# A 16 KB store of zeros, with two waits for it, at the start of a streaming subtract-the-mean kernel

## The chip, the cores and the metric

One core of one Trainium2 chip. The metric is the device time of one execution in microseconds (us); medians of several executions are given. Most executions of this kernel agree within some 0.3 us. The span of a profile is about 2 us shorter than the time of the same execution; times are compared with times and spans with spans.

## The reference

```python
B, S, D = 8, 4096, 2112          # x: float32
x_r = x.reshape(B, S // 4, 4, D)
pooled = x_r.mean(axis=2)
return x - np.repeat(pooled, 4, axis=1)
```

Four consecutive rows form a group; the mean of the group is taken from each of its rows. There are 8192 groups of 4 x 2112 = 8448 numbers. The kernel reads 276.8 MB and writes 276.8 MB.

## The kernel before

A tile is 128 groups, one per partition: 128 rows of 33,792 bytes. There are 64 tiles and six tile buffers ("slots"). SP (the sync engine) issues all loads, DVE (the vector engine) makes three adds and one fused subtract per tile, ACT (the scalar engine) issues all stores; SBUF and PSUM are the two on-chip memories. A load waits until the store that last used its slot has landed; the first six loads wait for nothing.

```python
for k in range(n):                                   # n = 64
    b, lap = k % SLOTS, k // SLOTS                   # SLOTS = 6
    load = nc.sync.dma_start(out=slots[b][:], in_=xg[k * P:(k + 1) * P])
    if lap:
        load._wait_ge(store_sems[b], 16 * lap)
    load.then_inc(load_sems[b], 16)
# ... DVE: for each tile three adds into s (s_sb in SBUF for even slots, s_ps in PSUM
#     for odd ones); the first add waits for load_sems[b]; then
#     slot = slot - s / 4, which raises done_sem ...
for k in range(n):
    b = k % SLOTS
    store = nc.scalar.dma_start(out=og[k * P:(k + 1) * P], in_=slots[b][:])
    store._wait_ge(done_sem, k + 1)
    store.then_inc(store_sems[b], 16)
```

## Time and profile before

| | before |
|---|---|
| time | 1284.66 us (6 runs beside the changed kernel, 1284.61 to 1284.79) |
| profiled span | 1283.3 us |
| DMA engines | full in all 40 slices |
| DVE | busy 80%, first add at 13.32 us |
| first store issued | 29.50 us |

The lines behind the table are in the prediction. One more view: what SP's loads wait for. Columns: who waited, for what, microseconds in total, how often, the longest.

```profile
SPq L85 <- DMA out_dram<-slot: 1169.0, 58, 50.7
```

Of the 64 loads 58 wait for a store to land, which makes the six slots a closed ring: load, compute, store, load again. While any load or store is queued, the 16 DMA engines have work.

The trace also holds the start, duration and size of every DMA packet. I sort the data packets by start and average each successive 16 of them, since 16 engines work side by side. In the kernel before, the median step from one such average to the next is 1.247 us: the time of one 33,792-byte row on one engine. 1024 rows per engine at 1.247 us are 1276.9 us of the 1283.3 us span, so the engines set the time.

### The profile page before, as it was taken

Reading aid. Unit: us, or ns where it says so; the run is one execution under the profiler, and the core shown is the slowest. Engines: PE = TensorE matmul, PEld = TensorE weight load, DVE = VectorE, ACT = ScalarE, POOL = GpSimd, SP = SyncE. Lnnn points to the kernel's source line nnn. Section 1 sums busy time; section 2 is a strip of 40 time slices with the busy share of each in tenths; the row PEclk is TensorE's granted clock in tenths of the full one; section 3 lists DMA queues with packets and bytes.
Section 4 is the critical chain, followed back from the end, with each engine's and each line's share of the span. In section 5 each row is a group of like instructions: output and inputs, shape, how many; then the busy total and the mean of one; then the engine's idle time right before and its main releaser. Section 6 shows DMA issues by size and latency. Waiting matters only on the chain.

```text
span 1283.3 us, 483 instructions
## 1 busy us (share of the span) xinstructions
DVE 1026.5 (80%) x256; POOL 0.2 (0%) x4
## 2 busy tenths in 40 slices
DVE  5998788787887877878778787787877878878785
POOL 0000000000000000000000000000000000000000
DMA  9999999999999999999999999999999999999999
GB/s 404 420 436 429 434 437 434 427 437 436 427 436 437 434 427 437 436 427 436 437 433 428 437 436 426 437 437 433 428 437 434 428 437 437 432 429 437 434 427 404
DMA packets 18432, 553.66 MB, mean 431 GB/s; under 512 B 2048, under 2 KB 2048, under 8 KB 2048
## 3 DMA queue, kind: packets, MB, share of 16 engines
q1 hardware_dynamic: 9216, 276.83, 50.1%
q10 hardware_dynamic: 9216, 276.83, 50.0%
HBM read 276.82 MB, written 276.82 MB: 431 GB/s over the span
## 4 chain that ended last, share of the span: by engine, by line
DVE 73%; another core or an unknown queue 24%; DMA 1%; issue 1%; DVEq 0%; SPq 0%
DVE slot L69 38%; DVE s_ps L63 18%; DVE s_sb L63 18%; DMA slot<-in_x_dram 1%; DVEq L90 0%; SPq L133 0%; SPq L82 0%
## 5 line engine op out<-in xcount | busy, mean ns | idle before, releaser
L69 DVE SCALAR_TENSOR_TENSOR slot<-s_sb,slot 128x8448 f32<-128x8448 f32 x32 | 286.7, 8958 | 1.1
L69 DVE SCALAR_TENSOR_TENSOR slot<-s_ps,slot 128x8448 f32<-128x8448 f32 x32 | 286.6, 8957 | 1.1
L63 DVE TENSOR_TENSOR s_sb<-slot 128x2112 f32<-128x2112 f32 x32 | 75.5, 2358 | 123.7 <-DMA slot<-in_x_dram 123.7
L63 DVE TENSOR_TENSOR s_ps<-slot 128x2112 f32<-128x2112 f32 x32 | 75.7, 2367 | 112.1 <-DMA slot<-in_x_dram 112.1
L63 DVE TENSOR_TENSOR s_ps<-s_ps,slot 128x2112 f32<-128x2112 f32 x64 | 151.4, 2366 | 2.2
L63 DVE TENSOR_TENSOR s_sb<-s_sb,slot 128x2112 f32<-128x2112 f32 x64 | 150.9, 2358 | 2.2
L122 POOL MEMSET const-bfloat16-1.0<- 128x1 bf16 x1 | 0.1, 102 | 0.0
L122 POOL MEMSET const-uint8-127<- 128x1 uint8 x1 | 0.1, 102 | 0.0
L122 POOL MEMSET const-float32-0.0<- 128x1 f32 x1 | 0.1, 99 | 0.2 <-issue 0.2
L122 POOL MEMSET const-float32-1.0<- 128x1 f32 x1 | 0.1, 99 | 0.0
## 6 DMA issues: line engine op xcount, KB each, us to landing
slot<-in_x_dram SPq DMA_DIRECT2D x64, 4224.0 KB, 60.1
out_dram<-slot ACTq DMA_DIRECT2D x64, 4224.0 KB, 43.5
```

The lines of the kernel that those rows point to most:

```text
L63: add = nc.vector.tensor_add(out=s[:], in0=first, in1=rows[:, f, :])
L69: sub = nc.vector.scalar_tensor_tensor(out=rows, in0=s[:, None, :].to_broadcast([P, STRIDE, D]), scalar=-1.0 / STRIDE, in1=rows, op0=mybir ...
L122: nc = _bacc.Bacc("TRN2", target_bir_lowering=False, num_devices=1)
```

## The change

A store of 32 rows of 512 bytes of zeros goes out first, into rows that the first tile's store overwrites. ACT waits for it to land before its first tile store (two writes to the same rows must not race), and DVE waits for it before its loop (it is going to overwrite the zeros in `s_sb`). The result is the same. Presumably the intent is to have the store queue used once before it matters; the code doesn't say.

```diff
+OPEN_ROWS, OPEN_COLS = 32, 128
 ...
+    open_sem = tc.alloc_semaphore("open")
+    opened = tc.alloc_semaphore("opened")
     with tc.tile_critical():
+        zeros = s_sb[:OPEN_ROWS, :OPEN_COLS]
+        nc.vector.memset(zeros, 0.0).then_inc(open_sem)
+        small = nc.scalar.dma_start(out=og[:OPEN_ROWS, :OPEN_COLS], in_=zeros)
+        small._wait_ge(open_sem, 1)
+        small.then_inc(opened, 16)
+        nc.scalar.wait_ge(opened, 16)
+        nc.vector.wait_ge(opened, 16)
         for k in range(n):
```

## The prediction

> **What bounds the kernel now.** I read the page first, then the waits, then the timeline of the first 70 us and a table of busy time by stretch. On the page the digits over 40 slices, the queues and the first DVE groups carry the reading:
>
> ```profile
> span 1283.3 us, 483 instructions
> DVE 1026.5 (80%) x256; POOL 0.2 (0%) x4
> DMA  9999999999999999999999999999999999999999
> GB/s 404 420 436 429 434 437 434 427 437 436 427 436 437 434 427 437 436 427 436 437 433 428 437 436 426 437 437 433 428 437 434 428 437 437 432 429 437 434 427 404
> DMA packets 18432, 553.66 MB, mean 431 GB/s; under 512 B 2048, under 2 KB 2048, under 8 KB 2048
> q1 hardware_dynamic: 9216, 276.83, 50.1%
> q10 hardware_dynamic: 9216, 276.83, 50.0%
> L69 DVE SCALAR_TENSOR_TENSOR slot<-s_sb,slot 128x8448 f32<-128x8448 f32 x32 | 286.7, 8958 | 1.1
> L63 DVE TENSOR_TENSOR s_sb<-slot 128x2112 f32<-128x2112 f32 x32 | 75.5, 2358 | 123.7 <-DMA slot<-in_x_dram 123.7
> ```
>
> The 16 DMA engines are full from the first slice to the last: the two queues' shares add up to 100.1% of 16 engines' span. Of the 18432 packets 2048 are tiny (the completion writes: 128 transfers by 16), so 16384 carry data, 1024 on each engine, and 1.001 x 1283.3 us / 1024 = 1.254 us is the mean time of one packet of 33,792 bytes (one row of a tile). DVE is busy 80% and waits for loads in between, so it isn't the bound. The chain of waits gives 73% to DVE; that is only the last link of each wait, and I overrule it with the DMA row, because the gaps on that chain are waits for transfers.
>
> The opening decides whether the change can touch anything. The timeline from 0 to 70 us:
>
> ```profile
> 0.95 53.96 SPq L85 DMA_DIRECT2D slot<-in_x_dram  x7
> 13.32 2.36 DVE L63 TENSOR_TENSOR s_sb<-slot 128x2112 f32<-128x2112 f32 x1 [13.32 <-DMA slot<-in_x_dram]
> ...
> 20.50 8.96 DVE L69 SCALAR_TENSOR_TENSOR slot<-s_sb,slot 128x8448 f32<-128x8448 f32 x1
> ...
> 29.50 32.45 ACTq L100 DMA_DIRECT2D out_dram<-slot  x3
> ```
>
> Loads start at 0.95 us, DVE is idle until 13.32 us, and ACT has no store to issue before 29.50 us. Everything that the change adds for DVE and ACT falls into these two idle stretches. The seventh load, the first that needs a store to have landed, is the last of the seven in the first line and goes out at about 0.95 + 53.96 = 54.9 us. The table by stretch shows that the engines don't run dry meanwhile:
>
> ```profile
> 0.00:10.00 10.00, 0.00 (x0) 0.20 (x4) 1.00 0.82 328
> 10.00:20.00 10.00, 6.61 (x3) 0.00 (x0) 1.00 1.00 433
> 30.00:40.00 10.00, 9.90 (x4) 0.00 (x0) 1.00 1.05 412
> 40.00:50.00 10.00, 9.97 (x3) 0.00 (x0) 1.00 1.00 433
> 50.00:60.00 10.00, 9.93 (x3) 0.00 (x0) 1.00 1.02 439
> ```
>
> The last two columns are DMA share and GB/s. Share 1.00 at 433 GB/s is the steady rate; the only dip inside is 412 GB/s in 30 to 40 us, when the first store joins the loads.
>
> **What the Trainium skill says.** (1) "DMA: Bandwidth & Descriptors", section "Where 436 GB/s comes from", puts the ceiling of a core's 16 ports at 435 GB/s. The trace agrees: 433 GB/s in full stretches. So there is no room for a faster kernel with the same bytes. (2) The same page, "Queues, rings and completion order": each engine alternates between queues with work, packet by packet. The trace agrees in its totals, 50.1% and 50.0% for the two queues, and the first store, issued at 29.50 us while loads were queued, had landed by 54.9 us, 25.4 us later. A store of 4224 KB (4.325 MB) at half of 433 GB/s takes 20.0 us; behind the queued loads it would have landed far later. (3) The same page, "Why a DMA increments its semaphore by 16 and not by 1": 32 rows are dealt to 16 engines, so two rows of 512 bytes and one completion write on each. (4) The same page, "Anatomy of one DMA", gives a fixed cost of about 2.0 us, mostly the receipt of the last write, for another path of issue than this one; the trace's nearest thing is the first load, issued at 0.95 us and seen at 13.32 us, 12.4 us where 4.325 MB at 433 GB/s take 10.0 us, so 2.4 us over the bytes. I use 2.4.
>
> **The change, part by part.** Nothing is removed and nothing is reordered: the comparison of the instruction streams shows one memset ahead of DVE's loop and one small store ahead of ACT's 64; the order on SP is the same.
> - Memset of 32x128 on DVE: four memsets of 128x1 on POOL take 0.1 us each; I take 0.1 to 0.2 us. It lies in the idle 13.32 us. Cost on the path: 0.
> - Small store: issued by ACT at some 1 to 2.5 us, after the memset. Each engine must pass two data packets and a completion write, with a load's packet of 1.254 us ahead of each: 3 x 1.254 = 3.8 us, plus 2.4 us fixed, plus up to one more packet already begun: 6 to 8 us. Landing at 8 to 10 us after the start. Estimate.
> - ACT's wait for it: over at 8 to 10 us, needed at 29.50 us: at least 19 us spare. Cost 0.
> - DVE's wait for it: over at 8 to 10 us, first load there at 13.32 us: 3 to 5 us spare. Cost 0. Should it miss by a few us, DVE and the first store start that much later, but two or more loads are still queued when the first store lands (54.9 - 2 us at 433 GB/s moved 22.9 MB, 5.3 tiles, of which at least one was a store and so at most 4.3 loads of 6). The engines have some 15 us or more of loads left, so a miss of a few us costs 0 too.
> - Engine time: 16 KB in all at 433 GB/s is 0.04 us. Small packets cost more than their bytes; I put two data packets and one completion write at 0.1 us each at most: 0.3 us on every engine, and this is on the path, since the engines are full to the end.
> - The joining of a second queue: the dip to 412 GB/s over 10 us, against 433, is 10 x 21 / 433 = 0.5 us lost once. The small store makes such a join early. If that loss is that of a queue's first use, it is only moved (0); if it is that of every join of a write stream, it is paid twice (+0.5 us). I count half: 0.25 us.
>
> Sum: 0.04 to 0.3 us of packets, say 0.15, plus 0.25 us: +0.4 us, so 1284.61 + 0.4 = 1285.0 us.
>
> **The rivals.**
> *All hidden:* the small packets fit into gaps of the first 2 us, before the loads' data flow (the first stretch has share 0.82). Then 1284.6. For it: the store is issued about as early as the loads; against it: it needs the memset and a semaphore first, and the loads' first packets will be ahead.
> *The small store waits behind whole loads:* if it lands only after the six free loads, 6 x 10.0 = 60 us, DVE starts at about 62 instead of 13 us. The engines would then have nothing from 62 until the first tile is done, 16.1 us later (29.50 - 13.32), so some 16 to 20 us are lost: 1301 to 1305 us, still only 1.3 to 1.6% slower. Against it: the 25.4 us of the first store. This is why I give slower by over 2% so little: even this failure doesn't reach it.
> *The engines keep a lasting change:* the two streams get another phase, the time of a packet moves. DVE has about 4 us of slack in 20 us a tile, and six slots keep both queues fed, so a phase has nothing to starve. One per cent in the packet time would be 12.8 us. Nothing in the profile speaks for it, and the packet time is that of the ports.
> *A gain from warming the stores' queue:* at most the 0.5 us of the dip, giving 1284.1.
>
> **Range and chances.** All hidden or warmed gives 1284.1 to 1284.6, my sum 1285.0, twice a join with dear packets 1286. Runs of the kernel before differ by 0.2 us. I take 1283.8 to 1286.8 for 8 in 10. Faster by over 2% means under 1258.9 us; moving 553.66 MB in that time needs 440 GB/s from first to last, above the 433 of a full stretch: 0.01. Slower by over 2% means over 1310 us, more than the worst story I can tell: 0.02. Within 2%: 0.97.
>
> **What the profile after would show.** Right: two DMA packets more on each engine (18432 + 48 = 18480 packets), one memset early on DVE, the small store landing before DVE's first add, which still starts at 13.3 us or within 1 us of it, the first big store still issued near 29.5 us, shares of the queues still about 50% each, and the steady stretch at 433 GB/s. Wrong step "two packets behind at most three load packets": DVE's first add would come later than 13.3 us, and its wait would be laid to the small store. Wrong step "queued loads cover a delay": the DMA row would show digits under 9 before 100 us. Wrong on the lasting rate: slices in the middle away from 427 to 437 GB/s. The prediction falls if the small store changes how the engines share the two queues for the rest of the run, which no view of the kernel before can show.

## The result and the profile after

The changed kernel took 1284.99 us (median of 6, 1284.87 to 1285.36) against 1284.66 us for the kernel before. The ratio is 1.0003 with a 95% interval of 0.999 to 1.0016: the same time. In microseconds the interval runs from 1.3 below to 2.1 above, so the 0.3 us between the medians is not an effect by itself.

The page of the changed kernel, the lines that answer to those of before. A digit is the busy share of one of 40 slices of the span, in tenths (9 is 90% or more). A queue's line gives packets, MB and share. An instruction group's line gives, after the first bar, busy microseconds and mean nanoseconds of one, and after the second the engine's idle time before it and what ended it. The last line gives the store's size and the microseconds from issue to landing.

```profile
span 1282.8 us, 486 instructions
DMA  9999999999999999999999999999999999999999
GB/s 405 421 438 427 433 438 434 426 438 437 423 438 438 428 432 438 436 424 438 438 421 438 438 428 432 438 436 424 438 438 423 437 438 429 431 438 436 424 438 405
DMA packets 18480, 553.67 MB, mean 432 GB/s; under 512 B 2064, under 2 KB 2096, under 8 KB 2096
q1 hardware_dynamic: 9216, 276.83, 50.1%
q10 hardware_dynamic: 9264, 276.84, 50.0%
L64 DVE TENSOR_TENSOR s_sb<-slot 128x2112 f32<-128x2112 f32 x32 | 75.4, 2357 | 122.7 <-DMA slot<-in_x_dram 122.7
L89 DVE MEMSET s_sb<- 32x128 f32 x1 | 0.2, 165 | 1.0 <-SPq L85 1.0
out_dram<-s_sb ACTq DMA_DIRECT2D x1, 16.0 KB, 8.3
```

There are 48 packets more, 32 of data and 16 completion writes: two rows and one completion on each engine. The DMA row is unchanged. The idle time ahead of the first adds into `s_sb` is still laid to the loads (122.7 us, before 123.7). The last line is the one to remember: the small store took 8.3 us from issue to landing.

The profiled execution is shorter here (1282.8 us) than before (1283.3 us), against the medians. By the packet records the rows keep the same pace (1278.1 us from the first average to the last before, 1278.0 after); what differs is the end: of the last 16 rows to finish, the last ends 0.66 us after the median one before, 0.18 us in the changed kernel and 0.26 us in its repeat. So a few rows that finish late move a single execution by tenths of a microsecond, with or without the change.

Its timeline of the first 60 us (start, duration, instruction):

```profile
0.95 53.61 SPq L98 DMA_DIRECT2D slot<-in_x_dram  x7
1.02 0.17 DVE L89 MEMSET s_sb<- 32x128 f32 x1 [1.02 <-SPq L85]
1.22 0.43 ACTq L90 DMA_DIRECT2D out_dram<-s_sb  x1
13.29 2.36 DVE L64 TENSOR_TENSOR s_sb<-slot 128x2112 f32<-128x2112 f32 x1 [12.11 <-DMA slot<-in_x_dram]
...
29.46 32.45 ACTq L113 DMA_DIRECT2D out_dram<-slot  x3
```

Issued at 1.22 us, landed 8.3 us later, at 9.5 us. DVE needs it at 13.29 us at the earliest and ACT at 29.46 us, and both instants are where they were (13.32 and 29.50 us). Everything that was added lies in time when those two engines had nothing to do.

The packet records show how the small store passes. Times are from the first data packet, itself at 1.95 us of the span; the packets named are the first on their turn among 16 engines:

```
time us   queue   bytes   duration ns
 3.076    loads   33792   1251
 4.323    stores    512     27
 4.347    loads   33792   1251
 5.594    stores    512     27
 5.617    loads   33792   1251
 6.864    stores      4      9      (completion write)
 6.870    loads   33792   1251
 8.117    loads   33792   1251
```

Loads and the small store take turns: one row of a load (1.247 us), one small packet, and so on. On an engine the small store costs 27 + 27 + 9 ns = 0.063 us. It waited through three rows of loads before its first turn; why three is not shown.

### The profile page after: what moved, and what is told of

Read it like the earlier page. It is cut to its first block, busy times and chain, and to the rows that moved or that the text cites. A ratio compares the mean times of both kernels' runs of the same rounds, so it can differ in the third digit from the quotient of the medians.

```text
span 1282.8 us, 486 instructions
## 1 busy us (share of the span) xinstructions
DVE 1026.6 (80%) x257; POOL 0.2 (0%) x4
## 4 chain that ended last, share of the span: by engine, by line
DVE 73%; another core or an unknown queue 24%; DMA 1%; issue 1%; DVEq 0%; SPq 0%
DVE slot L70 38%; DVE s_ps L64 18%; DVE s_sb L64 18%; DMA slot<-in_x_dram 1%; DVEq L103 0%; SPq L146 0%; SPq L85 0%
## 5 line engine op out<-in xcount | busy, mean ns | idle before, releaser
L64 DVE TENSOR_TENSOR s_sb<-slot 128x2112 f32<-128x2112 f32 x32 | 75.4, 2357 | 122.7 <-DMA slot<-in_x_dram 122.7
```

Source lines behind the costliest of these rows:

```text
L64: add = nc.vector.tensor_add(out=s[:], in0=first, in1=rows[:, f, :])
```

## The experiments

The theory: **the store and both waits are hidden, because the DMA engines have queued loads to work on and DVE and ACT have slack; only 0.06 us of engine time is paid.** The rivals: the join of the store queue is paid a second time; DVE's wait is on the path; the store is simply cheap and its place doesn't matter; any delay of DVE's start is paid in full. The runs were made in three sets, each set on one chip with runs of the kernel before beside it.

### The changed kernel again

No edit.

> The changed kernel unaltered, to size its difference finely. Theory 'hidden': the waits end at about 9.5 us, before DVE's first add at 13.3 us, so only the engine time of the small packets is paid, 2 x 27 ns + 9 ns = 0.06 us on each engine by the packet records of the profile: 1284.7 to 1285.0 us. Rival 'a second join of the write queue is paid' (half of it is in my prediction): +0.5 us, 1285.2 us or more, and the records would show a stretched packet when the small store comes in.

Measured: 1285.08 us (1284.96 to 1285.20) beside 1284.99 us of before: a difference of 0.09 us, where the first set of runs had 0.33. The ratio is 1.0001 (0.9987 to 1.0015). The packet records show no stretched step when the small store comes in: the two steps are 1.247 + 0.024 us. The rival of a second join, +0.5 us, gets no support in either.

### DVE doesn't wait

```diff
-        zeros = s_sb[:OPEN_ROWS, :OPEN_COLS]
+        zeros = pad[:OPEN_ROWS, :OPEN_COLS]      # a tile nobody else uses
-        nc.vector.wait_ge(opened, 16)
```

> The zeros come from another tile, so DVE no longer waits for the small store; ACT still does. Theory 'hidden': the wait was over before the first load landed, so nothing changes: the same time as the changed kernel within 0.3 us, first add at 13.3 us. Rival 'DVE's wait is on the path': faster than the changed kernel by 0.3 us or more, with the first add earlier.

Measured: 1285.02 us beside 1285.08 us of the changed kernel in the same rounds. The first add in that run's profile and in this one's:

```profile
13.44 2.36 DVE L64 TENSOR_TENSOR s_sb<-slot 128x2112 f32<-128x2112 f32 x1 [12.25 <-DMA slot<-in_x_dram]
13.53 2.36 DVE L64 TENSOR_TENSOR s_sb<-slot 128x2112 f32<-128x2112 f32 x1 [12.34 <-DMA slot<-in_x_dram]
```

It is no earlier without the wait, and in both it waits for the load. DVE's wait costs nothing that can be seen.

### The loads wait for the small store

```diff
             load = nc.sync.dma_start(out=slots[b][:], in_=xg[k * P:(k + 1) * P])
+            if k == 0:
+                load._wait_ge(opened, 16)
```

> The first load waits for the small store to land, so nothing lies beside it. Theory 'the store costs its latency where nothing covers it': issue at 1.2 us plus an unloaded landing of 2 to 3 us, so loads start at 3.5 to 4.2 us instead of 0.95 us: +2.5 to +3.3 us, 1287.2 to 1288.0 us. Rival 'the store is cheap by itself, not hidden': under 1286 us.

Measured: 1286.86 us beside 1284.80 us, +2.06 us. The interval of the ratio (1.0000 to 1.0033) just touches one, but the fastest of the four runs (1286.75 us) is above the slowest of the seven of before (1285.23 us), and the trace shows the delay. The issue of the small store and the loads' start on this run's timeline:

```profile
1.22 0.39 ACTq L90 DMA_DIRECT2D out_dram<-s_sb  x1
2.69 113.62 SPq L98 DMA_DIRECT2D slot<-in_x_dram  x10
```

and the store's line among the DMA issues of its page (the last number is the time from issue to landing):

```profile
out_dram<-s_sb ACTq DMA_DIRECT2D x1, 16.0 KB, 1.5
```

With nothing beside it the store lands in 1.5 us, and the loads start 2.69 - 0.95 = 1.74 us later. So the expectation was too high by some 0.5 us, since it put an unloaded landing at 2 to 3 us, but the store is plainly not free in itself: where nothing covers it, its latency is paid. And 1.5 against 8.3 us shows that most of the landing time in the changed kernel is waiting for turns behind rows of loads. A long landing is thus a sign that something else is being moved in the meantime.

### The same at the end

The memset, the store and ACT's wait are put ahead of the last tile's store, into the last tile's rows; DVE has nothing to wait for there.

```diff
-        # the seven lines at the beginning
+        blank = nc.vector.memset(zeros, 0.0)         # after the last tile
+        blank._wait_ge(done_sem, n); blank.then_inc(open_sem)
 ...
+            if k == n - 1:
+                small = nc.scalar.dma_start(out=og[k * P:k * P + OPEN_ROWS, :OPEN_COLS], in_=zeros)
+                small._wait_ge(open_sem, 1); small.then_inc(opened, 16)
+                nc.scalar.wait_ge(opened, 16)
```

> The same memset, store and wait of ACT, but ahead of the last tile's store instead of the first's (DVE's own wait is dropped, as it has nothing left to do). ACT has no slack there: the memset runs after the last big DVE instruction at about 1268.9 us, and the last store goes out only after the small one has landed. Theory 'place decides': the small store queues behind what is left of the store before it, lands some 4 to 8 us after its issue, and the engines go empty for 3 to 6 us: 1288 to 1291 us. Rival 'such a store costs only its packets wherever it is': 1284.7 to 1285.2 us.

Measured: 1286.84 us beside 1284.80 us, +2.04 us (interval of the ratio 0.9999 to 1.0033, but all four runs, 1286.61 us and up, above all seven of before). The expectation of 1288 to 1291 us was missed: the store landed 3.7 us after its issue, where 4 to 8 were expected, and the engines stood empty for 1.9 us and not for 3 to 6. But it is not the 0.1 us of the beginning either. The timeline of the end of this run:

```profile
1268.27 0.17 DVE L104 MEMSET s_sb<- 32x128 f32 x1
1268.47 0.34 ACTq L112 DMA_DIRECT2D out_dram<-s_sb  x1
1272.22 0.36 ACTq L117 DMA_DIRECT2D out_dram<-slot  x1
```

Its table by stretch, the last two columns being DMA share and GB/s:

```profile
1270.00:1275.00 5.00, 0.00 (x0) 0.00 (x0) 1.00 0.66 280
```

and the same stretch of the changed kernel:

```profile
1270.00:1275.00 5.00, 0.00 (x0) 0.00 (x0) 1.00 1.02 439
```

The last store goes out 3.75 us after the small one. Part of that was still covered by the rest of the store before it; for about a third of these 5 us the engines are empty, and the packet records show one step that is 1.86 us longer than a row. The same edit that hides at the beginning shows at the end, because no load is left to fill the gap.

### Eight, twelve, sixteen and twenty-four small stores

The same store several times, into different parts of the first tile, with both waits for all of them. This makes DVE's start as late as one likes.

```diff
+        COPIES = 8          # 12, 16, 24
+        for i in range(COPIES):
+            r, c = OPEN_ROWS * (i % 4), OPEN_COLS * (i // 4)
+            small = nc.scalar.dma_start(
+                out=og[r:r + OPEN_ROWS, c:c + OPEN_COLS], in_=zeros)
+            small._wait_ge(open_sem, 1); small.then_inc(opened, 16)
-        nc.scalar.wait_ge(opened, 16)
-        nc.vector.wait_ge(opened, 16)
+        nc.scalar.wait_ge(opened, 16 * COPIES)
+        nc.vector.wait_ge(opened, 16 * COPIES)
```

> Eight small stores (different rows and columns of the first tile) instead of one, one memset, both waits for all eight. Each store passes three packets per engine with a load packet ahead of each, 3 x 1.265 = 3.8 us, so the last lands at about 9.5 + 7 x 3.8 = 36 us and DVE starts there, 23 us late. Theory 'queued loads cover the delay': the loads last until about 63 us, the first store is issued at about 52 us; cost 8 x 0.063 = 0.5 us of packets and up to 3 us of refill gaps, 1285.2 to 1288 us. Rival 'a late start of DVE is paid in full': +23 us, about 1307 us.

> Twelve small stores. The last lands at about 9.5 + 11 x 3.8 = 51 us, so the first tile is done at about 67.5 us, some 4 us after the loads have run out at about 63 us. Theory 'queued loads cover the delay until they run out': 5 to 13 us lost (the gap, then gaps while the first stores and loads alternate), 1290 to 1298 us. Rival 'paid in full': +38 us, about 1323 us. Rival 'never paid': 0.8 us of packets, 1285.5 us.

> Twenty-four small stores. If each round keeps a load packet ahead, the last lands at about 9.5 + 23 x 3.8 = 97 us; once the loads run out at 64 us the rest go faster, since nothing alternates with them, so the landing may come at 66 to 75 us instead. Theory: the first tile is done 16 us after that, the engines are empty from there: 20 to 35 us lost, 1305 to 1320 us if the rest go fast, up to 1342 us if they don't. Rival 'paid in full' with a landing at 97 us: +84 us, 1369 us.

> Sixteen small stores, both waits. From 8 to 12 stores the landing moved from 33.9 to 46.7 us, 3.2 us a store, so DVE starts at about 59.5 us, 46 us later than before. With twelve and twenty-four stores the delay less the loss was 28 us. Theory 'a delay is free up to some 28 us and paid in full beyond': 46 - 28 = 18 us lost, 1301 to 1306 us. Rival 'paid in proportion to the number of stores' (25 us for 24): 16.6 us, so about the same, but a straight line is already ruled out by eight (2.5) and twelve (5.6).

Measured, each beside the kernel before in its own rounds. The delay is the start of DVE's first add less 13.32 us:

| stores | first add | delay | time | before | loss | delay less loss |
|---|---|---|---|---|---|---|
| 8 | 33.87 | 20.6 | 1287.53 | 1284.99 | 2.5 | 18.1 |
| 12 | 46.69 | 33.4 | 1290.36 | 1284.80 | 5.6 | 27.8 |
| 16 | 60.51 | 47.2 | 1304.40 | 1285.09 | 19.3 | 27.9 |
| 24 | 65.96 | 52.6 | 1309.70 | 1284.80 | 24.9 | 27.7 |

(One of the four runs with twelve stores took 1296.44 us; the other three were within 0.9 us.) From twelve stores on, the last column is constant: the loss is the delay less about 28 us, and each further microsecond is paid in full. (The delay is of one profiled run and the loss of medians. With the profiled runs' own times, the last column reads 18.0, 27.6, 29.0 and 25.8, so the agreement to 0.2 us is luck; within some 3 us it is constant.) Sixteen stores were run last, with the loss of 18 us worked out beforehand from this rule. Paid in full, twelve stores would have cost 33 us and not 5.6. The wait that was never seen in the changed kernel is now in the list of waits, and it is largest in the run with twenty-four:

```profile
DVE s_sb L64 <- DMA out_dram<-s_sb: 64.8, 1, 64.8
```

Where the 28 us come from, the table by stretch of that run shows:

```profile
50.00:60.00 10.00, 0.00 (x0) 0.00 (x0) 1.00 1.00 431
60.00:70.00 10.00, 4.00 (x2) 0.00 (x0) 1.00 0.32 128
70.00:80.00 10.00, 9.93 (x3) 0.00 (x0) 1.00 0.00 0
80.00:90.00 10.00, 9.90 (x5) 0.00 (x0) 1.00 0.75 324
```

For 60 us DVE does nothing and the engines run at full rate all the same, on the six free loads. Then those are used up and no store is ready until DVE has been through a tile. By the packet records the last row of the six loads starts at 62 us, and the step after it is 0.4 us longer than a row with twelve stores, 14.1 with sixteen and 19.4 with twenty-four. The delay less this one gap is 32.9, 33.1 and 33.2 us: so the queued loads cover 33 us of delay, near the 34 us from the first store's issue in the kernel before (29.50 us) to their end. Most of the other 5 us, which bring 33 down to 28, are shorter stretches just after, when few transfers are queued: in the run with twelve they add 2.2 us at 73 to 77 us, 0.8 at 81 to 84 and 0.9 at 112 to 117 (the kernel before loses 1.0 us at its one such place), and the small packets another 0.8. So most of the loss with twelve stores is of this kind, and only 0.4 us of it is the gap at the end of the loads. The page of the run with twenty-four shows that little is lost later: its third digit and rate fall, and its last slice is a little lower (8 and 370 GB/s, before 9 and 404).

```profile
DMA  9949999999999999999999999999999999999998
GB/s 400 404 182 411 428 429 439 434 429 430 439 434 431 429 437 437 431 429 434 439 432 429 432 439 434 429 430 439 435 429 430 439 434 431 430 436 436 432 430 370
```

Eight stores don't fit the rule so neatly: 20.6 us of delay should be free, and their packets are 8 x 0.063 = 0.5 us, but 2.5 us were lost. So a delay that the queued loads cover is not quite free.

### Eight stores, DVE not waiting

The run with eight stores, with the zeros in the unused tile and without DVE's wait, as in the second experiment.

> Eight small stores as before, zeros from another tile, and DVE doesn't wait for them; ACT still does. With DVE's wait the run took 1287.5 us, 2.5 us over before. Theory 'the rest of it comes from DVE's late start, not from the packets': DVE starts at 13.3 us, ACT's wait ends near 34 us, 4 us after the first tile is ready, while loads are queued; only the packets are paid, 8 x 0.063 = 0.5 us: 1285.3 to 1285.9 us. Rival 'each small store costs about 0.3 us by itself': 1287.5 us again.

Measured: 1286.37 us beside 1285.09 us, +1.3 us; the first add is back at 13.60 us. This is neither expectation: half of the 2.5 us goes with DVE's wait, half stays. For the half that goes, the records of the run with eight stores have a place: no load packet starts between 73 and 79 us, then the loads come back, and at some 88 us, soon after ACT had issued its third tile store at 82.2 us, two steps were 0.34 and 0.63 us longer than 1.247. That looks like a second joining of full-size stores to running loads; without DVE's wait the loads never pause for more than 1.7 us, and these steps are not there. Of the half that stays, 0.5 us is packets. Of the other 0.8 us the records place the larger part at the very end: of the last 16 rows the last ends 1.24 us after the median one, against 0.66 us in the kernel before. Why rows end late is not shown, and this is one profile each.

### A wide opening store

```diff
-OPEN_ROWS, OPEN_COLS = 32, 128
+OPEN_ROWS, OPEN_COLS = 128, 2112
```

> The opening store made 128 rows of 8448 bytes: 1.08 MB. At 433 GB/s its bytes are 2.5 us of all engines; it lands at about 20 to 22 us (nine packets on each engine, about 1.55 us a round, after 4 to 6 us), so DVE starts some 8 us late. Theory 'hidden but for engine time': 1284.7 + 2.5 = 1287.2 us, the DVE delay costs nothing. If the stretched packets at the first store's joining (1.0 us in the records of before) belong to the first use of the queue, they come at 4 to 6 us here and are gone at the first tile's store; if they belong to every start of full-size stores beside loads, they stay at the first tile's store.

Measured: 1288.92 us (1288.16 to 1289.69) beside 1284.99 us, +3.9 us where 2.5 was expected. It landed at about 21 us as expected (issue at 3.30 us, 17.7 us to landing; DVE's first add at 21.20 us, 7.9 us late). The records give 0.39 us per packet of 8448 bytes from start to start, so eight of them cost 3.1 us and not 2.5. Over the whole run the rows take 2.6 us longer than before, since the stretch at the first tile's store is smaller (next sentences); and of the last 16 rows the last ends 1.72 us after the median one, against 0.66 us before. The two together are near the 3.6 us by which the profiled span is longer. On the stretched steps at the first tile's store: in the kernel before they add 0.96 us, in the changed kernel 0.80, in its repeat 0.88, with loads waiting 0.92; here 0.36, and 0.19 at the wide store's own joining. So 512-byte rows don't take this cost away, and a wide store perhaps takes part of it; why the steps stretch at all stays open. The wide store costs far more than it could gain.

## Why the prediction was right

Predicted 1285.0 us, measured 1284.99; the range and "within 2%" hold. Step by step:

- **The bound.** Right. Mean rate 432 against 431 GB/s, the digits unchanged, the median step 1.247 us in both (so the rival of a lasting change falls), and every experiment that left the engines with queued work took the time of its packets and 2 us more at most. (16 rows in 1.247 us are 433.6 GB/s; the 437 and 439 GB/s of single stretches that the prediction shows, above its ceiling of 435, are presumably the coarseness of the bins, since one of them stands beside a share of 1.02.)
- **The memset.** Right: 0.17 us, at 1.02 us, off the path.
- **The landing at 8 to 10 us.** Right in the sum, 9.5 us, by luck: its parts were wrong. I had three to four rows of loads pass, at most two of them ahead of the first small packet; five passed, three of them ahead of it (first small packet at 6.27 us). I had 2.4 us of fixed latency; the small store's whole latency with nothing beside it is 1.5 us. The two errors nearly cancelled: 8.3 us from issue to landing, where 6 to 8 were forecast.
- **ACT's and DVE's waits cost 0.** Right, and shown: without DVE's wait the time is the same, and both engines start their work where they did before (for ACT's wait, which no run takes out, this is the evidence). "A miss of a few us costs 0 too" was not tested by itself: by the runs with eight stores, with and without DVE's wait, a delay of 20.6 us cost 1.2 us. Its working has a slip: it leaves 1.7 loads and says "two or more"; by the records 4.1 loads had moved by 54.9 us, so 1.9 were left.
- **The packets, 0.04 to 0.3 us.** Right at the low end: 0.063 us on each engine, from the records.
- **The joining of a second queue, 0.25 us.** This is the term that was mis-sized. The small store joined at no cost beyond its packets, so it wasn't paid twice, and the cost at the first tile's store wasn't taken away: 0.80 and 0.88 us in two profiles of the changed kernel, 0.96 in the one of before. This is no change: the run with the store at the end opens as the kernel before does, and shows 0.76. The rival of a gain from warming the queue falls with it. The dip read from the table by stretch made it 0.5 us once; from the records it is nearer 1 us, in both kernels. A better sum would have been +0.06 us.
- **Which difference is real.** The medians differ by 0.33 us in one set of rounds and by 0.09 us in another. The records explain 0.06. The rest lies inside the interval of each set, and I don't claim it. That 1285.0 was met to 0.01 us is therefore luck: the +0.4 us in it is mostly a term that wasn't there.

Of the rivals, "all hidden" was the closest, though the reason given for it was not: the small packets didn't fit into gaps of the first 2 us, they came at 6.3 to 8.8 us between rows of loads. "Waits behind whole loads" fell with the landing of 8.3 us; but the runs with sixteen and twenty-four stores show the failure that it described, an engine-empty stretch after 60 us; it named 16 to 20 us of loss, and they lost 19.3 and 24.9.

## What to carry to other kernels

Before pricing an added wait, ask what the busiest resource has queued while the wait lasts: here a wait until 9.5 us was free, a start of DVE 20.6 us late cost 1.2 us, and from about 33 us late, with the queued loads used up, each further microsecond cost one. The same small store cost 2 us where the queue was empty, at the very beginning with the loads held back or at the very end. A long time from issue to landing isn't a cost by itself; it can mean that the engines are well fed.

## What the Trainium skill lacked or had wrong

- "DMA: Bandwidth & Descriptors", section "Anatomy of one DMA", gives about 2.0 us of fixed cost for the other path of issue. A 16 KB store issued from ACT landed in 1.5 us with nothing beside it and in 8.3 us beside queued loads; the section has no figure for a landing under load.
- The same page, "Queues, rings and completion order", says that a queue drains a packet of typically 9 to 17 descriptors before the engine turns to the next. Here one row was one turn, of 33,792 bytes (1.247 us) for the loads and of 512 bytes (0.027 us) for the small store, and the new queue got its first turn after three rows of loads.
- I found no page with the stretch at the start of full-size stores beside running loads: 0.76 to 0.96 us once per run in the kernels that open with no store or the small one, 0.36 us after a wide opening store.
